# A list scheduler with longer handovers, and an interleaved last layer, in an eight-core decoder trunk

## The chip, the cores and the metric

The kernel runs on all 8 cores of one Trainium2 chip. Each core takes one of 8 prompts and 16 of 128 sample sequences, and the weights are the same for all. The metric is the time of the slowest core in device microseconds; lower is better. Some executions fall into a slower state, in which the cores of one die show a lower granted clock.

## The reference, cut to what matters

```python
def trunk(x, p, pool_bufs, conv_bufs, start, ...):
    h = x
    for i in range(DEPTH):                                   # 2 layers
        a = rmsnorm(h, norm_mix[i])
        u, bg, cg, v = split(a @ w_in[i])                    # 512 columns each
        y_pool = pool_mixer(u, ...)                          # windows of 2, 4, 8, 16, then a small matmul
        y_conv = bg * short_conv(cg * v, ...)
        h = h + concat(y_pool, y_conv) @ w_out[i]
        m = rmsnorm(h, norm_mlp[i])
        f = relu(m @ w_up[i]); h = h + (f * f) @ w_down[i]   # 1024 -> 4096 -> 1024
        gate = sigmoid(rmsnorm(h, norm_ple[i]) @ w_ple_gate[i])
        h = h + gate * (p[i] @ w_ple_proj[i])
    return rmsnorm(h, norm_f), ...
```

## The kernel before

The 2176 tokens of a core lie along the free dimension in five tiles of 512, 512, 512, 384 and 256 columns; the 1024 channels are 8 blocks of 128 partitions. The residual stream `h` stays in SBUF in float32, weights pass through a ring of 12 slots in bf16. Square sums over channels are made by a matmul with a matrix of ones.

The program doesn't write instructions in the order in which they run. It records operations with what they read and write, and a list scheduler in Python, with a small cost model, puts them in order for each engine at build time. Each engine gets its own list, with waits for semaphores in it. The scheduler's numbers and rules, before (numbers that the program assumes, not measurements):

```python
SEMLAT = 90.0        # ns from the end of a VectorE/ScalarE operation until others may use its result
PELAT = 190.0        # the same for TensorE
WINDOW = 40          # matmul groups among which the next one may be chosen
...
        for o in reversed(ops):                              # latest useful start, backwards
            a = min([s.alap for s in o.succ], default=t + 20000.0)   # t: end of the whole program
            ...
        for o in ops:                                        # whoever reads a bank may not be too late
            if o.ps is not None:
                for r in o.ps.readers:
                    r.alap = min(r.alap, ideal[o] + o.cost + 2500.0)
...
            else:
                vis[o] = end + SEMLAT                        # when the result counts as there
...
def c_dve(n, ap=False):                                      # cost of a VectorE operation, ns
    return 75.0 + 1.042 * n + (45.0 if ap else 0.0)
```

The last layer, before (cut):

```python
def rstd_of(ps, n, tw):                                      # (mean square + eps) ** -0.5
    P.op("act", ... func=AF.Ln, scale=1.0 / D, bias=EPS ..., kind="ln")
    P.op("act", ... func=AF.Exp, scale=-0.5 ..., kind="ln")
...
for t in range(NT):                                          # down stages d0 .. d4
    for c in range(KT):
        down(wd, c, t)
    ple_norm(l, t)
...
for t in range(NT):                                          # gate stages g0 .. g4
    ple(l, t, wu, wp)       # per 128 outputs: 8 + 2 matmuls, a sigmoid, a multiply, an add
    ...
    final(t)                # last norm, in place, and 4 stores of a quarter of the tile each
```

Of the kernel before, what the change touches and what calls it, by code (L numbers as in the profile page):

```python
# [13 lines left out]
D = 1024  # L14
# [19 lines left out]
NSLOT = 12  # L34

# [44 lines left out]
class Op:  # L80
    def __init__(self, i, eng, fn, cost):
        self.i, self.eng, self.fn, self.cost = i, eng, fn, cost
        self.deps = set()
        self.succ = []
        self.mms = None
        self.ps = None
        self.chan = None
        self.kind = None
        self.alap = None
        self.end = None  # L90
        self.fixed = None
        self.lead = 0.0


SEMLAT = 90.0
# [5 lines left out]
COLD = 15000.0  # L101


class Prog:
# [49 lines left out]
    def filler(self, lhsT, rhs, n, width, reads):  # L154

        o = Op(-1, "pe", None, 2.0 * n * width / 2.4)
        o.per, o.width, o.first, o.last, o.after = 2.0 * width / 2.4, width, True, True, None
        o.ps = Ps(self)
        ds = self._dep(o, reads, ())
        o.mms = [(lhsT, rhs, ds) for _ in range(n)]  # L160
        o.deps = set(ds)
        self.fillers.append(o)

    def mm(self, items, width, ps=None, last=True):

        o = Op(len(self.ops), "pe", None, 0.0)
        o.per = width / 2.4 + 2.6
        o.cost = o.per * len(items)
        o.width = width
        o.first, o.last = ps is None, last  # L170
        o.after = None
        if ps is None:
            ps = Ps(self)
        else:
            o.after = ps.group
            o.deps.add(ps.group)
        o.ps = ps
        ps.group = o
        o.mms = []
        for l, r, reads in items:  # L180
            ds = self._dep(o, reads, ())
            o.mms.append((l, r, ds))
            o.deps |= ds
        for _, _, reads in items:
            self._mark(o, reads, ())
        self.ops.append(o)
        return ps

    def schedule(self):
# [6 lines left out]
        for o in ops:  # L196
            if o.eng == "pe":
                ideal[o] = t
                t += o.cost
        for o in reversed(ops):  # L200
            a = min([s.alap for s in o.succ], default=t + 20000.0)
            lat = DMALAT if o.chan is not None else (PELAT if o.eng == "pe" else SEMLAT)
            dur = o.cost
            if o.chan is not None:
                dur += o.kind[1] / DMABW
            a -= dur + lat
            if o.eng == "pe":
                a = min(a, ideal[o])
            o.alap = a - o.lead if o.fixed is None else -1e9 + o.fixed
        for o in ops:  # L210
            if o.ps is not None:
                for r in o.ps.readers:
                    r.alap = min(r.alap, ideal[o] + o.cost + 2500.0)
# [11 lines left out]
        act_set = None  # L225
        vis = {}
# [25 lines left out]
        while left:  # L252
            best = None
            for e in self.ENGS:
# [27 lines left out]
                else:  # L282
                    bank = None
                    tau = max(free[e], min(ready[o] for o in cs))
                    pick = min((o for o in cs if ready[o] <= tau + 1.0), key=lambda o: (o.alap, o.i))
# [6 lines left out]
            cand[e].remove(o)  # L292
            dur = o.cost
# [30 lines left out]
    def emit(self):  # L324
# [13 lines left out]
        for e in self.ENGS:  # L338
# [18 lines left out]
            for o in self.order[e]:  # L357
                if o.mms is not None:
                    n = len(o.mms)
                    for j, (l, r, ds) in enumerate(o.mms):  # L360
                        ds = set(ds)
                        if j == 0 and o.prev is not None:
                            ds |= set(o.prev.readers)
                        w = waits_of(ds)

                        def f(eng, l=l, r=r, j=j, o=o, n=n):
                            return eng.matmul(self.psum[o.ps.bank][:, 0:o.width], lhsT=l, rhs=r,  # L367
                                              start=(o.first and j == 0), stop=(o.last and j == n - 1))
                        out.append((w, f, ("pe", 1) if j == n - 1 else None))
                else:  # L370
                    w = waits_of(o.deps)
                    out.append((w, o.fn, (o.chan, 16) if o.chan is not None else (e, 1)))
# [13 lines left out]
def build():  # L386
# [21 lines left out]
    with es:  # L408
# [34 lines left out]
        for k in range(KT):  # L443
            hB[k][0] = HA.buf(512 * k, 512 * k + 512)
            hH.append([HA.buf(512 * k + 256 * i, 512 * k + 256 * i + 256) for i in range(2)])
        m_ap = [[ab(blk(M0, t, k), TILES[t][1]) for k in range(KT)] for t in range(NT)]
# [4 lines left out]
        a_off = [M0 + 2 * W5, M0 + 3 * W5]  # L451
        x_off = [F0 + W5, F0]
# [108 lines left out]
        def rstd_of(ps, n, tw):  # L561
            P.op("act", lambda e: e.activation(out=rstd[:, n, 0:tw], in_=ps.ap()[:, 0:tw], func=AF.Ln, scale=1.0 / D, bias=EPS),
                 c_act(tw), ps=[ps], writes=[rsB[n]], kind="ln")
            P.op("act", lambda e: e.activation(out=rstd[:, n, 0:tw], in_=rstd[:, n, 0:tw], func=AF.Exp, scale=-0.5),  # L564
                 c_act(tw), reads=[rsB[n]], writes=[rsB[n]], kind="ln")
# [19 lines left out]
        def norm_stats(t):  # L585

            toff, tw = TILES[t]

            def add(a, b):
                P.op("dve", lambda e: e.tensor_tensor(out=sq[:, a:a + 2, 0:tw], in0=sq[:, a:a + 2, 0:tw], in1=sq[:, b:b + 2, 0:tw], op=ALU.add),  # L590
                     75.0 + 1.042 * tw, reads=sqB[a:a + 2] + sqB[b:b + 2], writes=sqB[a:a + 2])

            for k in range(KT):
                P.op("act", lambda e, k=k: e.activation(out=sq[:, k, 0:tw], in_=h[:, k, toff:toff + tw], func=AF.Square),  # L594
                     c_act(tw), reads=[hB[k][t]], writes=[sqB[k]])
                if k % 4 == 3:
                    add(k - 3, k - 1)
            add(0, 4)
            ps = P.mm([(ones[:], sq[:, q, 0:tw], [onesB, sqB[q]]) for q in range(2)], tw)
            n = st["rs"]  # L600
            st["rs"] = 1 - n
            rstd_of(ps, n, tw)
            return n
# [15 lines left out]
        def group(w, c, rhs, tw):  # L619

            ps = P.mm([(wk(w, c, k), rhs[k][0], [ringB[w.s], rhs[k][1]]) for k in range(KT)], tw)
            used(w)
# [175 lines left out]
        def ple(l, t, gate, wp):  # L798
            toff, tw = TILES[t]
            po, pB = PT_[t % 2]  # L800
            pt = ab(po, 2 * tw)
            for c in range(KT):
                p1 = group(gate[c // 2], c % 2, [(m_ap[t][k], mB[t][k]) for k in range(KT)], tw)
                p2 = P.mm([(ring[:, wp.s, kk * D + c * 128:kk * D + (c + 1) * 128], pt[:, kk * tw:(kk + 1) * tw], [ringB[wp.s], pB])
                           for kk in range(2)], tw)
                used(wp)
                ro, rB = R_[st["r"] % 3]
                st["r"] += 1
                P.op("act", lambda e, ro=ro, p1=p1: e.activation(out=af(ro, tw), in_=p1.ap()[:, 0:tw], func=AF.Sigmoid),  # L809
                     c_act(tw), ps=[p1], writes=[rB], kind="sig")  # L810
                P.op("dve", lambda e, ro=ro, p2=p2: e.tensor_tensor(out=af(ro, tw), in0=af(ro, tw), in1=p2.ap()[:, 0:tw], op=ALU.mult),  # L811
                     c_dve(tw), ps=[p2], reads=[rB], writes=[rB])
                P.op("dve", lambda e, ro=ro, c=c: e.tensor_tensor(out=h[:, c, toff:toff + tw], in0=h[:, c, toff:toff + tw], in1=af(ro, tw), op=ALU.add),  # L813
                     c_dve(tw), reads=[rB, hB[c][t]], writes=[hB[c][t]])

        def final(t):
            toff, tw = TILES[t]
            norm(t, V_NF, lambda k: h[:, k, toff:toff + tw], lambda k: hB[k][t])
            for k in range(0, KT, 2):
                P.dma("sp", lambda e, k=k: e.dma_start(out=y_t[:, k:k + 2, toff:toff + tw], in_=h[:, k:k + 2, toff:toff + tw]),  # L820
                      128 * 2 * tw * 4, f"y{t}_{k}", reads=[hB[k][t], hB[k + 1][t]])

        for l in range(DEPTH):
# [11 lines left out]
            for t in range(1, NT):  # L835
                mixer_in(l, t, w)
                mixer_out(t - 1, w)
                for n in ((t - 1,) if t < LT - 1 else (t - 2, t - 1) if t == LT else ()):
                    mlp_norm(l, n)
# [4 lines left out]
            for q in range(4):  # L844
                if q == 0:
                    for t in range(1, NT):
                        if t == 1:
                            mlp_norm(l, LT)
# [11 lines left out]
                else:  # L860
                    p_load(l, 0)
                    p_load(l, 1)
                    for t in range(NT):
                        for c in range(KT):
                            down(wd, c, t)
                        ple_norm(l, t)
                wu = [get() for i in range(4)]
            wp = get()
            for t in range(NT):
                ple(l, t, wu, wp)  # L870
                if t + 2 < NT:
                    p_load(l, t + 2)
                if l == DEPTH - 1:
                    final(t)
                elif t == 1 or t == 3:
                    rs = norm_stats(t // 2)
                elif t == 2 or t == 4:
                    mix_apply(l + 1, t // 2 - 1, rs)
# [113 lines left out]
```

## Time and profile before

| | before |
|---|---|
| time, median of 3 runs | 1516.46 us (1516.31 to 1518.2) |
| time, median of 12 runs, with those beside the changed kernel | 1516.66 us |
| profiled span of the cores | 1510.9 to 1514.5 us |
| granted clock of the cores | 0.993 to 0.996 |
| TensorE busy by the page | 1481.0 us |

### The profile page before, as it was taken

How to read it: one execution, taken by the hardware profiler on the slowest of the kernel's cores; microseconds unless marked ns; L12 is line 12 of the kernel's file. 1: busy time of each engine (PE TensorE's matmuls, PEld its weight loads, DVE VectorE, ACT ScalarE, POOL GpSimd, SP SyncE). 2: the span in 40 equal slices, each digit the busy share in tenths (PEclk: the TensorE clock that was granted, in tenths of full speed). 3: DMA queues.
4: the chain of work that ended last, by engine and by line, in shares of the span. 5: the costliest groups of instructions: out<-in, count | busy, mean ns of one | idle time of the engine just before them, and what ended most of it. 6: DMA issues, size and time to landing. Idle time of an engine off the chain costs nothing.

```text
span 1514.5 us, 24272 instructions; the slowest of 8 cores (1510.9 to 1514.5 us)
## 1 busy us (share of the span) xinstructions
PE 1481.0 (98%) x8082; PEld 785.1 (52%) x8082; DVE 928.9 (61%) x1770; ACT 531.2 (35%) x1016; POOL 64.6 (4%) x122
## 2 busy tenths in 40 slices
PE   7999999999999999999999999999999999999995
PEld 4444664555555555455544456565555555554543
DVE  5878885444444444488797987644444444446988
ACT  4444443003103103346644455320220230233686
POOL 3000010000000000000000001000000000000000
PEclk9999999999999999999999999999999999999998
DMA  9900172422221212104050007432222221200024
GB/s 190 221 19 1 26 126 44 70 42 33 39 42 30 42 28 43 29 1 63 13 88 0 1 1 124 68 57 42 30 41 39 33 43 28 43 1 1 1 83 170
DMA packets 26058, 75.61 MB, mean 50 GB/s; under 512 B 2512, under 2 KB 7376, under 8 KB 25904
## 3 DMA queue, kind: packets, MB, share of 16 engines
q0 software_dynamic: 17600, 60.69, 24.9%
q1 hardware_dynamic: 8192, 13.31, 2.6%
q8 instruction: 68, 1.11, 0.3%
q14 instruction: 54, 0.44, 0.1%
q10 hardware_dynamic: 144, 0.05, 0.0%
HBM read 118.28 MB, written 10.10 MB: 85 GB/s over the span
## 4 chain that ended last, share of the span: by engine, by line
PE 91%; DVE 3%; DMA 2%; issue 2%; ACT 1%; POOL 0%; DVEq 0%; ACTq 0%; SPq 0%; POOLq 0%
PE ps L367 91%; DMA ring<-w_in 2%; DVE arena L685 1%; DMA h<-x 1%; DVE sq L590 1%; DVE arena L693 0%; DVE h L608 0%; ACT sq L594 0%; DVE h L763 0%; DVE h L813 0%; ACT arena L668 0%; DVE arena L811 0%; POOL ring L537 0%; ACT arena L809 0%; POOL h L513 0%
## 5 line engine op out<-in xcount | busy, mean ns | idle before, releaser
L367 PE MATMUL ps<-arena,ring 128*128 128x512 bf16 (+2 forms) x7840 | 1454.4, 348 | 7.0 <-DMA ring<-w_in 4.3
L367 PEld LDWEIGHTS ps<-arena,ring 128*128 128x128 bf16 x7840 | 765.4, 98 | 683.4 <-issue 12.1
L763 DVE TENSOR_TENSOR h<-h,ps 128x512 f32<-128x512 f32 (+2 forms) x400 | 242.0, 606 | 256.2 <-PE ps L367 255.7
L778 ACT ACTIVATE arena<-ps 128x512 f32<-128x512 f32 (+2 forms) x320 | 170.4, 533 | 648.9 <-PE ps L367 627.7
L779 DVE TENSOR_TENSOR arena<-arena 128x512 bf16<-128x512 f32 (+2 forms) x320 | 195.0, 612 | 253.2 <-ACT arena L778 252.0
L594 ACT ACTIVATE sq<-h 128x512 bf16<-128x512 f32 (+2 forms) x272 | 145.6, 561 | 150.6 <-DVE h L763 117.0
L608 DVE SCALAR_TENSOR_TENSOR arena<-h,vec,rstd 128x512 bf16<-128x512 f32 (+2 forms) x232 | 145.3, 665 | 4.1 <-ACT rstd L564 3.9
L590 DVE TENSOR_TENSOR sq<-sq 128x1024 bf16<-128x1024 bf16 (+2 forms) x102 | 61.5, 606 | 19.3 <-ACT sq L594 17.9
L685 DVE TENSOR_TENSOR arena<-arena 128x526 f32<-128x526 f32 (+8 forms) x100 | 67.1, 671 | 3.5 <-ACT arena L668 2.0
L811 DVE TENSOR_TENSOR arena<-arena,ps 128x512 f32<-128x512 f32 (+2 forms) x80 | 47.0, 604 | 14.2 <-ACT arena L809 11.1
L749 DVE SCALAR_TENSOR_TENSOR arena<-arena,vec 128x512 f32<-128x512 f32 (+2 forms) x80 | 52.0, 676 | 5.3 <-ACT arena L745 3.8
L813 DVE TENSOR_TENSOR h<-h,arena 128x512 f32<-128x512 f32 (+2 forms) x80 | 46.7, 608 | 1.7
L809 ACT ACTIVATE arena<-ps 128x512 f32<-128x512 f32 (+2 forms) x80 | 40.6, 530 | 20.1 <-PE ps L367 12.8
L745 ACT ACTIVATE arena<-arena,vec 128x512 f32<-128x512 f32 (+2 forms) x40 | 30.0, 754 | 37.4 <-DVE arena L729 24.8
L537 POOL DMA_DIRECT2D ring<-w_up x32 | 16.9, 530 | 579.9 <-PE ps L367 579.2
L724 ACT ACTIVATE arena<-ps 128x512 f32<-128x512 f32 (+2 forms) x48 | 22.1, 472 | 46.2 <-DVE arena L716 28.6
L367 PE MATMUL ps<-sq,ones 128*128 128x512 bf16 (+2 forms) x84 | 22.3, 341 | 10.9 <-DVE sq L590 8.1
L537 POOL DMA_DIRECT2D ring<-w_down x32 | 16.9, 529 | 321.7 <-PE ps L367 320.4
L668 ACT ACTIVATE arena<-ps 128x512 f32<-128x512 f32 (+2 forms) x48 | 22.3, 469 | 21.2 <-PE ps L367 13.7
L729 DVE TENSOR_TENSOR arena<-arena,ps 128x512 f32<-128x512 f32 (+2 forms) x48 | 25.2, 529 | 5.1 <-ACT arena L724 2.8
L705 ACT ACTIVATE arena<-ps,vec 128x512 bf16<-128x512 f32 (+2 forms) x40 | 24.6, 618 | 7.6 <-PE ps L367 7.5
L693 DVE SCALAR_TENSOR_TENSOR arena<-arena 128x512 bf16<-128x512 f32 (+2 forms) x48 | 25.6, 534 | 2.6 <-PE ps L367 1.4
(43 smaller groups left out, 251.4 us busy)
## 6 DMA issues: line engine op xcount, KB each, us to landing
ring<-w_up POOLq DMA_DIRECT2D x32, 512.0 KB, 6.6
ring<-w_down POOLq DMA_DIRECT2D x32, 512.0 KB, 6.4
ring<-w_in POOLq DMA_DIRECT2D x16, 512.0 KB, 10.1
y_t<-h SPq DMA_DIRECT2D x12, 512.0 KB, 2.8
h<-x POOLq DMA_DIRECT2D x4, 1024.0 KB, 29.1
ring<-w_out POOLq DMA_DIRECT2D x8, 512.0 KB, 24.4
ring<-w_gate POOLq DMA_DIRECT2D x8, 512.0 KB, 6.3
h<-x SPq DMA_DIRECT2D x4, 512.0 KB, 8.7
```

The lines of the kernel that those rows point to most:

```text
L367: return eng.matmul(self.psum[o.ps.bank][:, 0:o.width], lhsT=l, rhs=r, start=(o.first and j == 0), stop=(o.last and j == n - 1))
L590: P.op("dve", lambda e: e.tensor_tensor(out=sq[:, a:a + 2, 0:tw], in0=sq[:, a:a + 2, 0:tw], in1=sq[:, b:b + 2, 0:tw], op=ALU.add), 75.0 + ...
L594: P.op("act", lambda e, k=k: e.activation(out=sq[:, k, 0:tw], in_=h[:, k, toff:toff + tw], func=AF.Square), c_act(tw), reads=[hB[k][t]], w ...
L608: P.op("dve", lambda e, k=k: e.scalar_tensor_tensor(out=dst(k), in0=h[:, k, toff:toff + tw], scalar=vcol(gbase + k), in1=rstd[:, n, 0:tw], ...
L685: P.op("dve", lambda e, to=to, src=src, v=v, sh=sh: e.tensor_tensor(out=af(to + v, ew - v), in0=af(src + v, ew - v), in1=af(src + v - sh, ...
L749: P.op("dve", lambda e, zo=zo, co=co, cwb=cwb, i=i: e.scalar_tensor_tensor(out=af(zo, zn), in0=af(co + i, zn), scalar=vcol(cwb + 4 * i), i ...
L763: P.op("dve", lambda e: e.tensor_tensor(out=h[:, c, toff:toff + tw], in0=h[:, c, toff:toff + tw], in1=ps.ap()[:, 0:tw], op=ALU.add), c_dve ...
L778: P.op("act", lambda e: e.activation(out=af(ro, tw), in_=ps.ap()[:, 0:tw], func=AF.Relu), c_act(tw), ps=[ps], writes=[rB])
L779: P.op("dve", lambda e: e.tensor_tensor(out=f_ap[t][c], in0=af(ro, tw), in1=af(ro, tw), op=ALU.mult), c_dve(tw), reads=[rB], writes=[fB[t] ...
L809: P.op("act", lambda e, ro=ro, p1=p1: e.activation(out=af(ro, tw), in_=p1.ap()[:, 0:tw], func=AF.Sigmoid), c_act(tw), ps=[p1], writes=[rB] ...
L811: P.op("dve", lambda e, ro=ro, p2=p2: e.tensor_tensor(out=af(ro, tw), in0=af(ro, tw), in1=p2.ap()[:, 0:tw], op=ALU.mult), c_dve(tw), ps=[p ...
L813: P.op("dve", lambda e, ro=ro, c=c: e.tensor_tensor(out=h[:, c, toff:toff + tw], in0=h[:, c, toff:toff + tw], in1=af(ro, tw), op=ALU.add), ...
```

## The change

It has four intents. The scheduler becomes more careful: a handover counts 300 ns instead of 90, stores and other last operations get deadlines near their place, readers of a bank are due earlier and pass this on. ScalarE changes its table set less often (31 table loads of 1.28 us in the trace before): the exponential follows its logarithm at once, and an operation of another set must be 2 us more urgent to be chosen. The gate stages of the last layer are interleaved with the down stages, two tiles behind, and the last tile takes another form: two outputs share a bank, and the sigmoid is made of exp, ln and exp, in the set of the norm. Finally the mixer's input and output swap regions, which lets some norms move, and stores cover half a tile.

```diff
+PIECES = [(0, 0, 512, False, "dve", "act", True), (1, ...), (2, ...),
+          (3, 0, 384, False, "dve", "act", True), (4, 0, 256, True, "dve", "act", False)]
+LAG = 2
...
-SEMLAT = 90.0
+SEMLAT = 300.0
...
+HOLD = 1000.0
+DUE = 20000.0
+STICK = 2000.0
...
         for o in ops:
+            o.due = t + DUE
             if o.eng == "pe":
                 ideal[o] = t
                 t += o.cost
+        for o in ops:
+            if o.ps is not None:
+                for r in o.ps.readers:
+                    r.cap = min(r.cap, ideal[o] + o.cost + HOLD)
         for o in reversed(ops):
-            a = min([s.alap for s in o.succ], default=t + 20000.0)
+            a = min([s.alap for s in o.succ], default=o.due)
+            a = min(a, o.cap + o.cost + SEMLAT)
...
+                    if e == "act" and forced is not None:      # the exponential right after its logarithm
+                        if forced not in cs:
+                            continue
+                        pick = forced
...
-        a_off = [M0 + 2 * W5, M0 + 3 * W5]
-        x_off = [F0 + W5, F0]
+        a_off = [F0, F0 + W5]
+        x_off = [M0 + 2 * W5, M0 + 3 * W5]
...
+                if not soft:
+                    P.op("act", ... func=AF.Sigmoid ...)
+                else:
+                    P.op("act", ... func=AF.Exp, scale=-1.0 ..., kind="ln")
+                    P.op("act", ... func=AF.Ln, bias=1.0 ..., kind="ln")
+                    P.op("act", ... func=AF.Exp, scale=-1.0 ..., kind="ln")
...
-            for k in range(0, KT, 2):
-                P.dma("sp", ...)                               # a quarter of a tile
+                if k % 4 == 3:
+                    P.dma("act" if (t, k) == (LT, 7) else "sp", ...)   # half a tile
...
+                    for t in range(NT + 1):
+                        if t < NT:
+                            for c in range(KT):
+                                down(wd, c, t)
+                            ple_norm(l, t)
+                        while nxt < len(PIECES) and (PIECES[nxt][0] <= t - LAG or t == NT):
+                            ...
+                            ple(u, wg, wp, c0, w, soft, eng)
+                            final(u, c0, w, sq_eng, adds)
```

## The prediction

> **What bounds the kernel now.** I read the clock per core first (all eight 0.993 to 0.996, spans 1510.9 to 1514.5 us, so nothing is slow or uneven), then the page.
>
> ```profile
> span 1514.5 us, 24272 instructions; the slowest of 8 cores (1510.9 to 1514.5 us)
> ...
> PE 1481.0 (98%) x8082; PEld 785.1 (52%) x8082; DVE 928.9 (61%) x1770; ACT 531.2 (35%) x1016; POOL 64.6 (4%) x122
> ...
> PE   7999999999999999999999999999999999999995
> ...
> DVE  5878885444444444488797987644444444446988
> ```
>
> TensorE is the bound: 1481.0 of 1514.5 us. Without fewer matmuls no change can win more than the other 33.5 us. The row of slices shows idle TensorE in the first and the last slice alone, and VectorE full at the end. Next, the waits of TensorE over the whole span:
>
> ```profile
> PE ps L367 <- DVE sq L590: 8.1, 7, 6.1
> PE ps L367 <- DMA ring<-w_in: 4.3, 2, 3.5
> PE ps L367 <- ACT sq L573: 2.3, 1, 2.3
> PE ps L367 <- DVE arena L693: 2.0, 5, 0.5
> ```
>
> Going through the timeline of TensorE alone I place the 33.5 us. About 10.8 are stalls before 40 us: the first squares, a small transfer and the first weights, the last stall 3.5 us on a weight transfer. About 5.5 are spread between 60 us and 1495 us in fifteen gaps of 0.15 to 0.77 us; only 0.36 lies at the layer boundary near 760 us. The rest is the tail. The busy time per stretch shows it:
>
> ```profile
> 1470.00:1480.00 10.00, 10.00 (x57) 5.37 (x56) 8.98 (x16) 8.30 (x14) 0.53 (x1) 1.00 0.27 67
> 1480.00:1490.00 10.00, 10.00 (x69) 6.61 (x68) 10.00 (x20) 8.89 (x16) 0.00 (x0) 1.00 0.34 129
> 1490.00:1500.00 10.00, 7.09 (x63) 5.79 (x60) 9.75 (x22) 8.77 (x17) 0.00 (x0) 1.00 0.36 133
> 1500.00:1515.00 15.00, 0.59 (x2) 0.13 (x2) 10.93 (x26) 4.85 (x12) 0.00 (x0) 0.54 0.70 247
> ```
>
> The columns after the width are TensorE, weight loads, VectorE, ScalarE, GpSimd. From 1480 us VectorE never rests, and TensorE runs out of work before it. The timeline of the tail says with what:
>
> ```profile
> 1495.03 2.56 PE L367 MATMUL ps<-arena,ring 128*128 128x256 bf16 x22
> ...
> 1496.94 2.73 DVE L608 SCALAR_TENSOR_TENSOR h<-h,vec,rstd 128x512 f32<-128x512 f32 x4
> 1497.08 0.49 ACT L562 ACTIVATE rstd<-ps 128x384 f32<-128x384 f32 x1
> 1497.58 1.28 ACT L809 ACT_TABLE_LOAD   x1
> ...
> 1502.26 1.28 ACT L564 ACT_TABLE_LOAD   x1
> ...
> 1503.56 0.52 ACT L564 ACTIVATE rstd<-rstd 128x384 f32<-128x384 f32 x1
> ...
> 1504.18 7.49 DVE L608 SCALAR_TENSOR_TENSOR h<-h,vec,rstd 128x384 f32<-128x384 f32 x16 [0.64 <-ACT rstd L564]
> ```
>
> The last matmul on weights ends at 1497.59 us, 16.9 us before the end. The log half of the fourth tile's reciprocal root is done at 1497.57, its exponential half 6 us later: ScalarE went back to sigmoids, with two table loads, and to the last tile's squares. So the final scaling of both last tiles, 16 instructions, runs as one block of 7.5 us after TensorE is done, and the last store lands 2.8 us after it.
>
> [...]The trace has 31 loads of 1283 ns[...]: a load at 1481.43 starts 0.02 us after the activation before it ended, and the next activation starts at 1482.72. I count 1.28. [...]the 512 KB stores here take 2.8 us from issue to landing[...].
>
> **The change part by part.** The matrix work is the same. The arithmetic is that of before except in the last tile of the last layer.
>
> (1) Last layer: before, all five output projections of the MLP (down), then five gate stages, each with its final norm. After, the gate stage of a tile follows two tiles behind: d0 d1 d2 g0 d3 g1 d4 g2 g3 g4. To see what this is worth, I set VectorE against TensorE. Rates in a row from the timeline: a 512-wide add or multiply 0.62, a scaled write 0.68 (2.73 for 4); at 384 wide 0.50 (1.49 for 3) and 0.54; at 256 wide 0.36 (1.09 for 3) and 0.40. A 512 down stage: 8 residuals, 3 square sums, 8 scaled writes = 5.0 + 1.9 + 5.4 = 12.3 us, against 64 matmuls at 0.2155 = 13.8. A 512 gate stage: 16 + 3 + 8 = 9.9 + 1.9 + 5.4 = 17.2 against 80 matmuls and two small ones = 17.7. The 384 gate stage: 13.8 against 13.4. The 256 one: 10.1 against 9.5. So VectorE has no slack in the gate stages, and falls behind in the last two, on top of whatever backlog it brings. Interleaving lets d3 and d4 (1.25 tiles, about 1.5 us of slack each) work off some of it: roughly 2 us less backlog at the end of TensorE.
>
> (2) The log is followed at once by its exponential, and ScalarE stays in a table set unless the other operation is 2 us more urgent. Loads: 18 in the last 155 us, 23 us of ScalarE. I expect about half, 14 to 18 in the whole kernel in place of 31. ScalarE is not the bound, so the 20 us are not gained; what counts is that the fourth tile's scaling (8 times 0.54 = 4.3 us) no longer waits 6 us. It can run during g4 and leave the tail.
>
> (3) The last tile: two 256-wide outputs share a bank, so one 512-wide instruction does the work of two. VectorE: 8 times 0.62 in place of 16 times 0.36, 0.8 us less; no square sums, 1.1 us less; TensorE does 8 small matmuls in place of 2, 6 times 0.117 = +0.7 us, most of it among the other matmuls. The sigmoid becomes exp, ln, exp: 3 passes of about 0.6 for 4 batches, 7.2 us in place of 8 times 0.32 = 2.6; it saves two or three loads (2.6 to 3.9 us), one of which would be in the last chain.
>
> (4) Stores of half a tile in place of a quarter, the last one on another queue: same bytes, the last one again 512 KB, 2.8 us. No gain.
>
> (5) Other regions for the mixer's input and output, moved norms (the one of tile 2 moves from the mixer into the up stage), and a scheduler with 300 ns in place of 90 for a handover, an earlier cap for reading a bank. These touch the 5.5 us of small gaps. A more cautious order should take away a part; I put 1.5 us on this, and 0.8 on the two gaps (0.77 and 0.51) in the old gate stages. The start is set by the weight transfers (the wait of 3.5 us that ends at 39.3 us), which don't change: 0.
>
> The new tail, from the last matmul on weights: first exp starts about 0.4 us before it (the projection of the embedding comes after the gate's); three passes 1.95; multiply and add 1.4 with the handover; square 0.7; the last small matmuls 0.6[...]; ln and exp 0.9 with handovers; 8 scaled writes 3.3; store 2.8. Sum 11.3 to 11.5 us with all engines free. They are not: ScalarE has in g4 four times 3 passes and a square (2.6 us a batch, 10.3), one load (1.3), the fourth tile's late squares (about 1.9) and its ln and exp (1.0), 14.5 us against 10.2 of TensorE. It will be about a microsecond later than the free chain, and VectorE's rest of tile 3 costs some tenths. I take 13.0 in place of 16.9: 3.9 less.
>
> Sum: -3.9 (tail) -0.8 (gaps in the gate stages) -1.5 (other gaps) +0.4 (small matmuls) = -5.8. 1516.5 - 5.8 = 1510.7; I put down 1510.5.
>
> **Rivals.** (a) ScalarE becomes the end: the soft sigmoid, one dependent pass after the other, keeps banks and the three result buffers occupied and TensorE stalls in g4. For it: 14.5 against 10.2 above. Against: eight banks hold all four batches. It would leave the tail at 15 to 17 us: 1514 to 1517. (b) VectorE stays the end: the interleaved order only moves its backlog, since its sum (some 90 us from g0 on) is within 5% of TensorE's 95. The last two tiles' writes again come as one block: 1513 to 1516. (c) All goes well: free tail of 11.5 and most small gaps gone: 1506 to 1507. (d) The new latency and the earlier caps upset the order in the mixer stages, where VectorE is 80 to 90% busy, and norms come late: TensorE stalls of some us in each layer, 1518 to 1525. The layer boundary has 20 us of gate work ahead of it, which speaks against a stall there.
>
> **Range and chances.** (c) and the free tail give the low end, (a) and (b) the high end: 1505.5 to 1516 should hold it 8 times in 10. A win of over 2% would need 30 of the 33.5 idle us, 10.8 of them in the start that isn't touched: 1 in 100. A loss of over 2% needs 30 us of stalls, or a weight block that comes late; the weights' order is the same and the gate's blocks find their slots free during the last up stage: 1.5 in 100.
>
> **What would show it.** TensorE's busy time within 2 us of 1481. The stretch before 40 us within 1 us. From the last matmul on weights to the end 11.5 to 14.5 us, with 8 scaled writes after the last exponential instead of 16. Table loads about halved. Small gaps between 60 us and the last gate stage below 4 us. It is wrong if TensorE shows waits of over 1 us on ScalarE or VectorE in the last 100 us (rivals a, b), if the mixer stages show new waits (d), or if the whole gain lies before 1400 us.

What no trace or run of this case shows is cut, and the cuts are marked. No term of the sum is among the cuts: it stands at -3.9 - 0.8 - 1.5 + 0.4 = -5.8 us. The trace before also shows when the loads come: 30 of the 31 are the 30 times that ScalarE goes between the sigmoid (L809) and the logarithm or exponential, and there is none in the 56 changes between logarithm and exponential. A 512-wide add or multiply of VectorE is drawn 0.68 to 0.69 us long.

## More of the kernel before

The page and the views that carry the argument are shown in the prediction. One line of the page that it does not show is the chain that ended last, as shares of the span by engine:

```profile
PE 91%; DVE 3%; DMA 2%; issue 2%; ACT 1%; POOL 0%; DVEq 0%; ACTq 0%; SPq 0%; POOLq 0%
```

Nine tenths of the time is matmuls, one behind the other. So the question for any change is where TensorE waits.

## The result, and the profile after

The changed kernel took 1504.99 us, median of 10 runs (eight fast ones, 1504.39 to 1505.99, and two slow ones of 1631 and 1794 us with one die at a clock of 0.82 to 0.93). Ratios are the mean time of one kernel's fast runs over that of the other's of the same rounds, so they are not quite ratios of the medians quoted. Here the ratio is 0.9922, interval 0.9912 to 0.9932. The prediction had 5.8 us of gain, and the range ended at 1505.5. The gain was 11.7 us, from 1516.66, twice as much.

The page after: span, busy time of the engines, and the chain that ended last.

```profile
span 1503.2 us, 24115 instructions; the slowest of 8 cores (1498.3 to 1503.2 us)
...
PE 1478.9 (98%) x8088; PEld 789.1 (52%) x8088; DVE 924.1 (61%) x1751; ACT 522.1 (35%) x980; POOL 64.7 (4%) x122
...
PE 96%; DMA 2%; DVE 0%; POOL 0%; ACT 0%; issue 0%; DVEq 0%; SPq 0%; ACTq 0%; POOLq 0%
```

TensorE is busy 2.1 us less although it runs six matmuls more. That can't be work; it is the first sign that "busy" hides waiting. The waits of TensorE after:

```profile
PE ps L389 <- DMA ring<-w_in: 4.6, 2, 3.1
PE ps L389 <- ACT sq L630: 4.6, 3, 3.0
PE ps L389 <- ACT sq L600: 2.1, 2, 1.8
PE ps L389 <- DVE arena L605: 1.7, 1, 1.7
PE ps L389 <- DVE arena L754: 1.5, 1, 1.5
PE ps L389 <- DMA poolw<-pool_w: 1.4, 1, 1.4
```

The second line is the tail, and all the others lie before 40 us. The five waits on VectorE's line of the pooling mixer (L693 before) and the six small ones on square sums are gone. The two mixer stages show it, as busy time by stretch: before, then after; the columns are those of the prediction's table, and in brackets stands the number of matmuls.

```profile
60.00:200.00 140.00, 138.34 (x743) 71.61 (x742) 120.62 (x264) 66.83 (x149) 4.79 (x9) 1.00 0.24 50
...
760.00:960.00 200.00, 197.80 (x1056) 102.22 (x1055) 172.65 (x376) 92.00 (x193) 7.40 (x14) 1.00 0.26 41
```

```profile
60.00:200.00 140.00, 140.00 (x762) 74.38 (x760) 121.76 (x269) 65.25 (x142) 4.80 (x9) 1.00 0.25 53
...
760.00:960.00 200.00, 200.00 (x1077) 105.23 (x1075) 168.51 (x369) 92.22 (x187) 7.41 (x14) 1.00 0.27 46
```

In the same 140 us, 19 matmuls more. Part of that is a different mix of widths, but idle time alone (1.66 us before) could not hold them.

**Counting the waits properly.** In the trace a 512-wide matmul is drawn 380 ns long, while in undisturbed stretches the next one starts 215.8 ns later (median 216; 162.5 at 384 wide, 109.2 at 256). A wait shorter than the difference, 0.16 us, leaves no gap at all, and each longer one is shown 0.16 us too short. So I took for every matmul the time from its start to the next start, less these 215.8, 162.5 or 109.2 ns, and call the sum "stalls". Summed from the point where 50 us of weight matmuls are done until the last matmul on weights; "start" is the same before that point; "tail" is from the end of the last weight matmul to the end of the span. Cores whose trace lacks matmul records are left out of the stalls.

| mean of the cores, us | before | after | difference |
|---|---|---|---|
| start | 15.7 (13.0 to 17.1) | 15.0 (12.1 to 17.9) | -0.7 |
| stalls | 10.2 | 0.2 | -10.0 |
| tail | 16.9 | 15.2 | -1.7 |
| span | 1513.3 | 1500.9 | -12.4 |

On core 0 before there were some 35 such stalls; 21 show as idle with 6.0 us in sum, the others don't show at all. The start varies from core to core by more than it changed, so I make nothing of its 0.7.

The tail after, as a timeline (start, duration, engine, line, operation):

```profile
1487.40 0.60 PE L389 MATMUL ps<-arena,ring 128*128 128x256 bf16 x4
1487.66 0.49 ACT L589 ACTIVATE rstd<-ps 128x384 f32<-128x384 f32 x1 [0.81 <-PE ps L389]
1488.25 0.52 ACT L591 ACTIVATE rstd<-rstd 128x384 f32<-128x384 f32 x1
1488.68 0.58 ACT L873 ACTIVATE arena<-ps 128x512 f32<-128x512 f32 x1
1488.87 1.68 DVE L888 SCALAR_TENSOR_TENSOR h<-h,vec,rstd 128x384 f32<-128x384 f32 x3 [0.31 <-ACT rstd L591]
...
1490.71 0.62 ACT L876 ACTIVATE arena<-arena 128x512 f32<-128x512 f32 x1
...
1492.97 1.23 ACT L630 ACTIVATE sq<-h 128x512 bf16<-128x512 f32 x2 [1.12 <-DVE h L880]
1493.40 2.20 DVE L888 SCALAR_TENSOR_TENSOR h<-h,vec,rstd 128x384 f32<-128x384 f32 x4
...
1495.50 0.42 ACT L591 ACTIVATE rstd<-rstd 128x256 f32<-128x256 f32 x1
1496.02 3.26 DVE L888 SCALAR_TENSOR_TENSOR h<-h,vec,rstd 128x256 f32<-128x256 f32 x8 [0.42 <-ACT rstd L591]
1499.36 0.41 ACTq L892 DMA_DIRECT2D y_t<-h  x1
```

As predicted, 8 scaled writes follow the last exponential, not 16, and the fourth tile's logarithm and exponential stand together. But the fourth tile's own eight scaled writes (384 wide) have not left the tail: on the two cores looked at (1 and 3) they run from 0.9 to 7.5 us after the last matmul on weights, 4.5 us of VectorE between the last batches' operations. And the last batch's first exponential starts 0.7 us after the last matmul, where the sum in the prediction had 0.4 us before it; its three passes take 2.65 us, with another batch's passes in between, not 1.95; multiply and adds take 2.15, not 1.4; and the last store needs 3.9 us to the end, not 2.8.

### The profile page after: what moved, and what is told of

Its sections match the earlier page's. It is cut to its first block, busy times and chain, and to the rows that moved or that the text cites. A ratio compares the mean times of both kernels' runs of the same rounds, so it can differ in the third digit from the quotient of the medians.

```text
span 1503.2 us, 24115 instructions; the slowest of 8 cores (1498.3 to 1503.2 us)
## 1 busy us (share of the span) xinstructions
PE 1478.9 (98%) x8088; PEld 789.1 (52%) x8088; DVE 924.1 (61%) x1751; ACT 522.1 (35%) x980; POOL 64.7 (4%) x122
## 4 chain that ended last, share of the span: by engine, by line
PE 96%; DMA 2%; DVE 0%; POOL 0%; ACT 0%; issue 0%; DVEq 0%; SPq 0%; ACTq 0%; POOLq 0%
PE ps L389 96%; DMA ring<-w_in 2%; DMA h<-x 1%; DVE h L888 0%; POOL ring L564 0%; POOL h L540 0%; DVE arena L877 0%; ACT rstd L591 0%; ACT rstd L589 0%; ACT sq L630 0%; DVE h L880 0%; POOL poolw L557 0%; SPq L533 0%; DVEq L430 0%; DVEq L982 0%
## 5 line engine op out<-in xcount | busy, mean ns | idle before, releaser
L818 ACT ACTIVATE arena<-ps 128x512 f32<-128x512 f32 (+2 forms) x320 | 170.5, 533 | 639.9 <-PE ps L389 623.7
L630 ACT ACTIVATE sq<-h 128x512 bf16<-128x512 f32 (+1 forms) x244 | 139.9, 601 | 115.4 <-DVE h L803 97.9
L877 DVE TENSOR_TENSOR arena<-arena,ps 128x512 f32<-128x512 f32 (+1 forms) x72 | 46.0, 654 | 10.1 <-ACT arena L870 9.7
L870 ACT ACTIVATE arena<-ps 128x512 f32<-128x512 f32 (+1 forms) x68 | 37.7, 572 | 33.4 <-PE ps L389 32.5
L880 DVE TENSOR_TENSOR h<-h,arena 128x512 f32<-128x512 f32 (+1 forms) x72 | 45.8, 657 | 1.8
L708 ACT ACTIVATE arena<-ps 128x512 f32<-128x512 f32 (+2 forms) x48 | 22.6, 472 | 36.6 <-PE ps L389 33.2
L764 ACT ACTIVATE arena<-ps 128x512 f32<-128x512 f32 (+2 forms) x48 | 22.4, 469 | 27.9 <-PE ps L389 20.8
L769 DVE TENSOR_TENSOR arena<-arena,ps 128x512 f32<-128x512 f32 (+2 forms) x48 | 25.4, 529 | 9.0 <-PE ps L389 8.1
L564 POOL DMA_DIRECT2D ring<-w_down x32 | 16.9, 529 | 322.3 <-PE ps L389 320.0
```

What stands on the lines that cost most here:

```text
L630: P.op("act", lambda e, hk=hk, qk=qk: e.activation(out=qk, in_=hk, func=AF.Square), c_act(w * nb), reads=hbs, writes=qB[k:k + nb])
L818: P.op("act", lambda e: e.activation(out=af(ro, tw), in_=ps.ap()[:, 0:tw], func=AF.Relu), c_act(tw), ps=[ps], writes=[rB])
L870: P.op("act", lambda e, ro=ro, p1=p1: e.activation(out=af(ro, m), in_=p1.ap()[:, 0:m], func=AF.Sigmoid), c_act(m), ps=[p1], writes=[rB], k ...
L877: P.op("dve", lambda e, ro=ro, p2=p2: e.tensor_tensor(out=af(ro, m), in0=af(ro, m), in1=p2.ap()[:, 0:m], op=ALU.mult), c_dve(m), ps=[p2], ...
L880: P.op(en, lambda e, ro=ro, hc=hc: e.tensor_tensor(out=hc, in0=hc, in1=af(ro, m).rearrange("p (c n) -> p c n", n=n), op=ALU.add), c_dve(m) ...
```

## The experiments

Eighteen kernels ran, all correct, with five rounds each. The table has stalls and tail from each one's profile; the text says what each one tells. The runs marked * were on a chip whose second die ran at 0.98 to 0.99 of the clock (in two slow executions at 0.83 and 0.97), and on which the kernel before took 1525 us; there stalls and tail are from cores 0 to 3, undisturbed (0.993 to 0.997), and the ratios are weaker evidence. On that chip the expected times can't be checked. For e6 the figures are those of seven cores; core 1 was slower in its last weight matmuls (the last 20 took 3.70 us, those of core 3 2.34), so that 1.2 us of its tail counts as stalls, 4.7 and 16.7.

| run | stalls | tail | time, median | ratio to before (95%) |
|---|---|---|---|---|
| before | 10.2 | 16.9 | | |
| after, repeated (e16) | 0.2 | 15.2 | 1503.88 | 0.9924 (0.9911 to 0.9938) |
| e1 before, new scheduler | 3.0 | 16.5 | 1509.42 | 0.9952 (0.9939 to 0.9964) |
| e2 after, old scheduler | 8.4 | 18.0 | 1515.83 | 0.9991 (0.9977 to 1.0004) |
| e3 before, 300 ns | 1.5 | 16.3 | 1507.5 | 0.9934 (0.9921 to 0.9948) |
| e4 after, 90 ns | 8.5 | 14.5 | 1513.56 | 0.9975 (0.9961 to 0.9988) |
| e5 after, not interleaved | 0.2 | 17.3 | 1505.9 | 0.9936 (0.9923 to 0.9949) |
| e6 after, last tile as before | 3.5 | 17.9 | 1511.67 | 0.9970 (0.9957 to 0.9983) |
| e7 after, quarter stores | 0.2 | 15.4 | 1504.59 | 0.9924 (0.9911 to 0.9937) |
| e8 after, old deadlines | 2.1 | 16.4 | 1506.98 | 0.9942 (0.9928 to 0.9955) |
| e9* after, old regions | 0.0 | 15.2 | 1518.68 | 0.9938 (0.9920 to 0.9956) |
| e10* after, no pairing, no staying | 0.0 | 18.6 | 1521.0 | 0.9968 (0.9953 to 0.9983) |
| e11* after, 200 ns | 0.6 | 14.6 | 1518.16 | 0.9949 (0.9935 to 0.9963) |
| e12* after, 600 ns | 0.4 | 18.7 | 1521.17 | 0.9964 (0.9948 to 0.9979) |
| e13 after, last store on the common queue | 0.2 | 14.6 | 1502.88 | 0.9920 (0.9904 to 0.9935) |
| e14 both: 200 ns, common queue | 0.6 | 14.0 | 1503.06 | 0.9920 (0.9907 to 0.9934) |
| e15 as e14, last tile in quarters | 0.6 | 14.0 | 1503.44 | 0.9923 (0.9909 to 0.9938) |
| e17 after, 300 ns to TensorE only | 5.4 | 14.6 | 1509.25 | 0.9955 (0.9942 to 0.9968) |
| e18 after, 300 ns among the others only | 0.2 | 14.6 | 1504.8 | 0.9925 (0.9913 to 0.9938) |

My theory after reading the two traces was that the order of instructions took away the stalls, and in it the one number for the handover. The rivals were the changed program, and the scheduler's other rules.

### e1 and e2: scheduler or program

```diff
 e1: the kernel before, with
+SEMLAT = 300.0, HOLD, DUE, STICK, the caps, the deadlines, the exponential after its logarithm
 e2: the changed kernel, with all of that taken back
```

> The kernel before with the whole new scheduler (300 ns handover, earlier caps on readers of a bank, deadlines of stores and other last operations near their place, log and exponential together, staying in a table set) and nothing of the changed program. Theory A (the order of instructions did the ten microseconds between the start and the last matmul on weights): the stalls of TensorE in that stretch fall from 10.2 to under 2 us, and the tail too gets shorter than 16.9 us, since the fourth tile's exponential no longer waits: 1504 to 1508 us. Rival B (the program did it: other regions, moved norms, the last layer interleaved): the stalls stay above 7 us, 1512 to 1517 us.

> The changed program (interleaved last layer, other regions, moved norms, last tile in pairs with the soft sigmoid, larger stores) under the whole old scheduler. Theory A: the stalls between start and last matmul stay at 6 to 11 us, tail 14 to 16 us: 1511 to 1516 us. Rival B: stalls under 3 us, 1504 to 1508 us.

The scheduler alone took the stalls from 10.2 to 3.0 us, a microsecond more than its expectation had. Most of the rest is in the last gate stages (one stall of 2.1 us there waits on a multiply that reads a bank). The time of 1509.4 lies between the two expectations. The program alone left 8.4 us of stalls, and its time differs from the kernel before by less than the interval. So the program without the scheduler gains nothing that can be told from noise, and its tail even got longer, 18.0 us; 5.2 us of it lie between the last write and the end, and 1270 KB were still left to store when the last store was issued (see e7 below).

### e3 and e4: one number

```diff
 e3: the kernel before, with            e4: the changed kernel, with
-SEMLAT = 90.0                          -SEMLAT = 300.0
+SEMLAT = 300.0                         +SEMLAT = 90.0
```

> The kernel before with one number changed, the scheduler's handover of 300 ns in place of 90. If the handover alone accounts for the stalls (theory A1): stalls of TensorE from 10.2 to under 2.5 us, tail about as before (16 to 17.5 us): 1507 to 1510 us. If it is the deadlines and caps (theory A2): stalls stay above 6 us, 1512 to 1517 us.

> The changed kernel with one number put back, the handover of 90 ns. Theory A1: stalls of TensorE go from 0.2 to 5 us or more, 1509 to 1515 us, tail about 15 us. Theory A2: stalls stay under 2 us, 1504 to 1507 us.

One number in the kernel before gives 9.4 us, where the whole change gave 11.7. In that program it leaves fewer stalls than the whole new scheduler does, 1.5 us beside the 3.0 of e1, so the other rules don't help there. The busy time of the mixer stages in e3:

```profile
60.00:200.00 140.00, 140.00 (x761) 74.37 (x760) 122.06 (x267) 70.16 (x152) 4.79 (x9) 1.00 0.25 53
...
760.00:960.00 200.00, 199.93 (x1076) 104.92 (x1074) 171.62 (x377) 95.19 (x197) 7.40 (x14) 1.00 0.27 44
```

and in e4:

```profile
60.00:200.00 140.00, 138.79 (x743) 71.94 (x742) 120.05 (x261) 64.71 (x141) 4.79 (x9) 1.00 0.24 50
...
760.00:960.00 200.00, 198.03 (x1061) 102.91 (x1060) 168.96 (x365) 88.49 (x180) 7.93 (x15) 1.00 0.25 43
```

The unchanged program with 300 ns has the 140.00 of the changed kernel and, with 761, all but one of its matmuls; the changed program with 90 ns has the 743 matmuls of the kernel before. What the number does can be seen at one of the longest stalls in the first mixer. Before (the lines between are of other work):

```profile
184.34 0.69 DVE L693 SCALAR_TENSOR_TENSOR arena<-arena 128x128 bf16<-128x128 f32 x2
...
185.17 0.27 PE L367 MATMUL ps<-arena,poolw 128*128 128x256 bf16 x1 [0.36 <-DVE arena L693]
185.29 3.65 PE L367 MATMUL ps<-arena,ring 128*128 128x256 bf16 x32
```

After:

```profile
181.96 3.66 PE L389 MATMUL ps<-arena,ring 128*128 128x256 bf16 x32
185.46 0.27 PE L389 MATMUL ps<-arena,poolw 128*128 128x256 bf16 x1
185.56 2.78 PE L389 MATMUL ps<-arena,ring 128*128 128x256 bf16 x24
```

The same small matmul of the pooling mixer was placed after 16 large ones and waited there (this stall: 0.53 us, of which 0.36 show); the 32 large ones behind it started after it, at 185.29. With 300 ns the scheduler put 32 large ones ahead of it, and its input was there. The order costs nothing, since the large ones have to be done anyway.

### e9 and e8: regions, deadlines

```diff
 e9: the changed kernel, with           e8: the changed kernel, with
+old regions, norms in their old place  +default=t + 20000.0, readers capped at +2500, not passed on
```

> The changed kernel with the mixer's input and output back in their old regions and the norms in their old places (also at the layer boundary). If the regions and moved norms matter: stalls of TensorE from 0.2 to over 1.5 us, 1506 to 1509 us. If not (the prediction gave them no number of their own): stalls under 1 us, tail 15.2, 1504 to 1506 us.

> The changed kernel with the old deadlines: last operations due at the end of the program instead of near their place, and readers of a bank capped late and without passing it on. If the deadlines matter for the tail: the final scaling of tiles 2 and 3 is put off again, tail 16 to 18 us, stalls before it under 2 us: 1505.5 to 1508.5 us. If only the handover matters: tail and stalls unchanged, 1504 to 1506 us.

The regions show no effect: stalls 0.0, tail 15.2 on the undisturbed die. The deadlines are worth 1.9 us of stalls and 1.2 us of tail, but their kernel's time (1506.98 beside 1504.59 of e7 on the same chip) sits just inside the noise of the start; the trace carries this verdict.

### e5, e6, e10: the parts of the last layer

```diff
 e5: -LAG = 2
     +LAG = 9                            # all d, then all g
 e6: -(4, 0, 256, True, "dve", "act", False)
     +(4, 0, 256, False, "dve", "act", True)    # one sigmoid per output, no shared banks
 e10: no forced exponential, STICK = 0
```

> The changed kernel with the interleaving of the last layer taken back: all five down stages, then the five gate stages (one number, the lag of 2 set to 9). Theory of the prediction: VectorE loses about 2 us of slack, tail 15.2 to about 17 us, stalls before it still under 1 us: 1506 to 1508 us. Rival (the interleaving earns nothing, since the tail is one chain through ScalarE and the last stores): tail within 0.5 us of 15.2, 1504 to 1506 us.

> The changed kernel with the last tile as before: one sigmoid per output, 256 columns each, square sums on VectorE. Theory of the prediction: the paired, soft form saves table loads and VectorE time, so without it the tail grows to 16.5 to 18 us: 1506 to 1508.5 us. Rival (a) of the prediction, that the three dependent passes make ScalarE the bound of the tail: the tail shrinks to 13.5 to 14.8 us, 1503 to 1504.5 us.

> The changed kernel without the pairing of log and exponential and without staying in a table set. The prediction held that the pairing takes the fourth tile's scaling out of the tail. If so the tail grows to 16.5 us or more and the table loads go from 23 back to 28 or more: 1506 to 1508 us. If the handover already does it, tail 14.8 to 15.8 us and stalls under 0.5 us: 1504 to 1506 us.

Interleaving is worth 2.1 us of tail, as the prediction worked out from VectorE's slack (about 2), and the traces show the backlog: the last tile's first multiply starts 2.3 us before the last matmul on weights in the changed kernel, and 0.4 us after it in e5 (core 1 of both). Pairing and staying in a table set, taken out together, are worth 3.4 us of tail: without them 33 table loads instead of 23, and ScalarE waits for VectorE in the last tile. It isn't the effect that was predicted: the fourth tile's writes run in the tail with them and without them, from 0.9 us after the last matmul on weights with them, from 5.4 us without. Two lines of e10's ScalarE, from an undisturbed core:

```profile
1488.99 0.60 ACT L873 ACTIVATE arena<-ps 128x512 f32<-128x512 f32 x1 [1.69 <-DVE h L880]
...
1494.11 0.63 ACT L630 ACTIVATE sq<-h 128x512 bf16<-128x512 f32 x1 [1.93 <-DVE h L880]
```

The first of these is an exponential that could not start before an add had freed one of the three result buffers; rival (a) of the prediction named them, and here they bite. That the missing pairing is what brought VectorE behind is argued from the order, not measured by itself; pairing and staying were not run apart.

The last tile's form is worth more than the prediction and the expectation had: 2.7 us of tail and 3.3 us of stalls. On the core looked at most closely 2.2 us of these stalls are in the last gate stage and 1.2 near the layer boundary, where the first layer's last tile goes back to single outputs too. TensorE in e6, in the last gate stage:

```profile
1485.61 0.48 PE L389 MATMUL ps<-sq,ones 128*128 128x384 bf16 x2 [1.43 <-DVE arena L877]
...
1486.81 2.34 PE L389 MATMUL ps<-arena,ring 128*128 128x256 bf16 x20 [0.49 <-ACT arena L870]
1496.90 0.59 PE L389 MATMUL ps<-sq,ones 128*128 128x256 bf16 x2 [7.75 <-DVE sq L621]
```

The first two waits are on readers of PSUM banks (the multiply and the sigmoid). Eight outputs with two banks each need 16 banks one after the other; in pairs they need eight, and eight (of 128x512 float32) is what the kernel sets up.

### e11 and e12: how large must the number be

```diff
 e11: -SEMLAT = 300.0  +SEMLAT = 200.0      e12: -SEMLAT = 300.0  +SEMLAT = 600.0
```

> The changed kernel with a handover of 200 ns. In the stalls of the kernel before, TensorE started 145 ns (fifteen of 21) or about 255 ns after the end of the instruction it waited for, and a VectorE instruction ends some 75 ns later than the scheduler's cost for it says, so the real handover is about 220 to 330 ns as the scheduler counts. Theory D (the number has to reach the real handover): at 200 most stalls are gone but not all, 0.5 to 4 us of stalls instead of 8.5 at 90 and 0.2 at 300: 1504 to 1509 us. Rival (any larger number merely reorders by luck): stalls anywhere between 0 and 10 us, not between those of 90 and 300.

> The changed kernel with a handover of 600 ns, twice what the traces show. Theory D: no stalls come back (under 0.5 us), and since the scheduler now believes that the chain of the last tile is longer than it is, the tail changes by under 1 us either way: 1504 to 1506.5 us. Rival (an exact number matters, too much slack costs as much as too little): stalls over 2 us, 1507 us or more.

(A correction to the first of the two: of the stalls looked at, eleven had VectorE's result 145 ns and six about 255 ns before, and three had ScalarE's 132 to 144 ns before.) Stalls 8.5, 0.6, 0.2, 0.4 us at 90, 200, 300, 600: nearly all of the fall lies between 90 and 200. That is in the range that theory D gave for 200, but below the 220 to 330 ns that it took for the real handover; four settings don't show whether there is a threshold. The tail answers differently, 14.5, 14.6, 15.2 and 18.7 us, which D did not expect: at 600 it is 3.5 us longer than at 300. With too long a handover the scheduler orders VectorE and ScalarE for delays that don't exist, and where there is no other work to put between, in the tail, the wrong order costs time. That last sentence is my reading; the runs show the numbers alone.

### e17 and e18: whose handover

```diff
 e17: 300 ns for results that TensorE waits for (and banks), 90 among the other engines
 e18: the reverse
 (both in the estimated times alone; the deadlines are worked out with 90 throughout in e17, 300 in e18)
```

> The changed kernel with 300 ns only where TensorE waits for a result of VectorE or ScalarE or for a bank to be read, and 90 ns among the other engines. If the number is needed for TensorE's own waits: stalls under 1.5 us, and the tail as at 90 (14.3 to 14.8 us): 1503 to 1505 us. If the chains among VectorE and ScalarE that lead up to it need it too: stalls of 2 to 6 us, 1506 to 1511 us.

> The complement: 90 ns where TensorE waits, 300 ns among the other engines. If TensorE's own waits need the number: stalls of 5 us or more, 1508 to 1514 us. If the chains do: stalls under 3 us, and a tail of 15 us or more.

Here my theory fell. I had measured that TensorE starts 145 or about 255 ns after the end of the VectorE operation that it waits for, and believed that these handovers needed the number. But 300 ns to TensorE alone leaves 5.4 us of stalls, and 300 ns among VectorE and ScalarE alone leaves 0.2. So the short estimate does its harm on the way to TensorE, and not at the last step. One thing the two runs don't separate: the pass that works backwards to the deadlines takes SEMLAT for every handover, those to TensorE too, so e17 has short deadlines and e18 long ones. Whether the estimated times or the deadlines need the longer number stays open; no run has the one without the other. Per link the trace has: VectorE's 512-wide operations start 602 ns apart when they follow each other, and each ends after 685, so a result is ready 83 ns later than a cost that fits the pace; and from the end on ScalarE to the start on VectorE it takes 102 ns (median of 329), the other way 95 (of 298), at times 170 to 270. That makes some 180 ns a link, up to 350, where the scheduler had 90. By this estimate an input of TensorE that comes over several links would be late by the sum. This fits the fall between 90 and 200 in e11, but the sum along one chain was not measured by itself. The tail of both halves is 14.6 us, against e18's expectation of 15 or more, so the 15.2 comes only with both.

### e7, e13, e14, e15: the last store

```diff
 e7: -if k % 4 == 3:  +if k % 2 == 1:                    # quarters, the last one still on ScalarE's queue
 e13: -P.dma("act" if (t, k) == (LT, 7) else "sp", ...)
      +P.dma("sp", ...)
 e14: e13 and SEMLAT = 200.0        e15: e14 and the last tile in quarters
```

> The changed kernel with stores of a quarter of a tile as before (half the bytes each, twice as many), the last one still on the other queue. In the changed kernel the last half-tile store takes 3.8 us from its issue to the end, where the quarter stores of the kernel before took 2.8. Theory C (the larger stores at the end cost what the prediction left out, they queue behind each other): tail 14.2 to 14.7 us, about 0.7 us faster. Rival: the store's time is the same whatever its size at this point: tail 15.0 to 15.4, no change.

> The changed kernel with its very last store issued from the same queue as all the others. Theory E (a store issued from ScalarE's queue takes about a microsecond more, whatever its size): last write to end 2.7 to 3.1 us instead of 3.9, tail 14.0 to 14.5 us. Rival (half a tile takes longer than a quarter, or waits behind the stores before it): 3.7 to 4.1 us as before, tail 15 to 15.4.

> Both the handover of 200 ns and the last store from the common queue. If the two gains in the tail add up: tail 13.3 to 13.9 us, stalls 0.4 to 0.9, in sum 1 to 1.5 us better than the changed kernel. Rival (one hides the other): tail 14.2 us or more.

> As the run before, and the last tile stored in quarters. If the size of the last store counts once the queue is the right one: last write to end 2.4 to 2.7 us, tail 13.0 to 13.5. If the stores are bound by the bytes left at that point, or by a fixed time: no change from the run before (within 0.2 us).

> The changed kernel once more, on the same chip as the three runs after it. Stalls 0.2 us, tail 15.2 us, ratio to the kernel before 0.991 to 0.994.

From the last write to the end: 3.9 us in the changed kernel, 4.1 with quarters (e7), 3.3 with the common queue (e13, e14), 3.3 with the common queue and the last tile in quarters (e15), 2.8 in the kernel before. So the queue accounts for 0.6 us, where theory E gave it about 1. The DMA packets in the traces show where the rest went (means of the eight cores; the store itself is counted in the KB that are left):

| | KB left when the last store is issued | last write to last packet, us | last packet to end, us |
|---|---|---|---|
| before | 676 | 2.2 | 0.7 |
| e1 before, new scheduler | 569 | 1.9 | 0.7 |
| e2 after, old scheduler | 1270 | 3.9 | 1.3 |
| after | 834 | 2.7 | 1.2 |
| e7 quarter stores | 567 | 1.9 | 2.2 |
| e13 common queue | 836 | 2.7 | 0.7 |
| e15 common queue, last tile in quarters | 830 | 2.7 | 0.7 |

The last packet comes later the more is left, from 1.9 us after the last write with 567 KB to 3.9 with 1270, which fits stores that wait behind each other, as theory C had it. The larger halves leave 834 KB in place of 676, which accounts for the 0.5 us that e13 still lacks to the kernel before. In e7 the data are through 0.8 us earlier (expected were 0.7), but on ScalarE's queue the end then comes 2.2 us after the last packet instead of 1.2, and the gain doesn't show; why stays open. In e15 the fourth tile's half store still lies ahead of the last tile's quarters. Quarters throughout on the common queue were not run in this program; e1, which stores like that, needs 2.6 us. The gains of queue and of 200 ns in the tail add up, 15.2 to 14.0 us, but 200 ns give 0.4 back in stalls. By the traces e14 is 0.8 us better than the changed kernel. By the clock it is not to be told from it: 1503.06 and 1503.88 us on the same chip, ratios 0.9920 and 0.9924 with intervals of 0.0013 to either side. The fault is the start, which differs by up to 6 us between cores of one run. A kernel with e18's numbers and the common queue was not run.

## Why the prediction was right or wrong

- **The bound** (TensorE, at most 33.5 us to win): the engine was right, the figure was not. It took "busy" as work. The trace of the kernel before shows otherwise: a 512-wide matmul is drawn 380 ns long, and the next one starts after 215.8. The same slip makes the 256-wide gate stage 9.5 us in part (1): at the pace of 109.2 ns it is about 9.0.
- **The step that failed** is "About 5.5 are spread between 60 us and 1495 us in fifteen gaps", together with part (5), "A more cautious order should take away a part; I put 1.5 us on this, and 0.8 on the two gaps". The pool was 10.2 us and all but 0.2 of it went: 10.0 us for a term of 2.3; by the one number for the handover alone 8.7 of 10.2 went (e3). About 4 us of the error is that hidden waiting; the other part is that I took a guess at the share instead of asking what the 90 ns stood for. The handovers could have been read from the trace of the kernel before, 180 ns and more against 90.
- **The tail**, 13.0 from 16.9, came out at 15.2: the direction and the eight writes after the last exponential were right, the size was not. The terms mis-sized are the late start of the last batch on ScalarE (1.1 us), its three passes (0.7), multiply and adds (0.75) and the store (1.1); the allowance of about 1.5 us for busy engines was too small by 2.2. The sum also left out the fourth tile's eight writes, 4.5 us of VectorE in the tail ("VectorE's rest of tile 3 costs some tenths"); how much of the delay they cause was not measured.
- **Part (1)**, about 2 us from interleaving: e5 has 2.1, and VectorE's later start on the last tile with it. Right.
- **Part (2)**, the fourth tile's scaling can "run during g4 and leave the tail": wrong. Its exponential comes at once, but all eight writes still follow the last matmul on weights; only the last block of 16 is cut to 8. The rules are worth 3.4 us all the same (e10), which by its size looks like the predicted 4.3 and is luck. The table loads fell to 23, not to 14 to 18.
- **Part (3)** was too small. It counted VectorE's and TensorE's time, and not the banks; e6 has 2.2 us of stalls on them in the last gate stage alone.
- **Part (4)**, the stores, "No gain": it is a loss of 1.1 us, 0.6 through the other queue (e13) and 0.5 through the larger stores ahead. "The last one again 512 KB" is wrong: the last tile's quarter was 256 KB, its half is 512. And 2.8 us is not the least seen: e1 needs 2.6.
- **The start** unchanged within 1 us: right for the mean.
- **The rivals**: of (a) the stalls in the last gate stage did not come, but a tail inside its 15 to 17 us did; (b) did not come, the last two tiles' writes are no longer one block. (d), that the new number upsets the mixer stages, is the opposite of what happened: they were where most was won. (c) came nearest in time, by another way: a tail 3.7 us longer than its 11.5, and some 5 us more of stalls gone than it counted.
- **Parts are not a sum.** Taken back one at a time, interleaving, pairing with staying, and the last tile's form cost 2.1 to 3.4 us of tail each, the deadlines 1.2, yet the whole change shortened it by 1.7 only. Losing any one of the first three brings the tail beyond the 16.9 us of before, to 17.3 to 18.6.

## What to carry to other kernels

Measure a saturated engine's waiting by the pace of its starts, not by gaps between drawn instructions: here 4 of 10 us of waiting lay under matmuls that looked busy. In a static schedule, put the handover in near what the trace shows from one engine's end to the next one's start, plus the tail of an instruction that its pace hides (here 95 to 102 ns, and 83); here too little (90 ns) cost 8.3 us of stalls, and twice as much (600 ns) 3.5 us of tail. And before giving a share to "a more cautious order", find the number that the order rests on and try that number alone: here it gave 9.4 us by itself, where the whole change gave 11.7.
